# A Mamba-2 scan in transposed layout: the normalisation of each head group put off into the next group, and the decay matrices kept in three fixed tiles

## The chip, the cores and the metric

The kernel runs on one NeuronCore of a Trainium2 chip. The core has five engines that run side by side, each through its own instructions in order: TensorE (PE, matrix products), VectorE (DVE), ScalarE (ACT), GpSimd (POOL) and SyncE (SP, which issues the loads of the weights). They wait for one another by semaphores. The metric is the device time of one launch in microseconds, the median of several runs.

## The reference

A trunk of two layers on one sequence of 256 tokens, model width 1024, all in float32. Each layer is an FFN, a token mixer and another FFN, each followed by a layer norm. The mixer of the first layer is a sparse attention; that of the second is a Mamba-2 SSD, to which the change belongs:

```python
def ssd_mixer(x, w_in, conv_w, conv_b, dt_bias, a_log, d_skip, norm_g, w_out):
    z, xbc, dt = jnp.split(x @ w_in, [SSM_INNER, SSM_INNER + SSM_CONV_DIM], axis=-1)
    ...                                   # causal conv of 4 taps over xbc
    xs, b_in, c_in = jnp.split(jax.nn.silu(conv), [SSM_INNER, SSM_INNER + SSM_GROUPS * SSM_STATE], axis=-1)
    ...
    y = ssd_scan(xs, dt, a, b_in, c_in)
    y = y + xs * d_skip
    yz = y.reshape(bsz, seq, SSM_INNER) * jax.nn.silu(z)
    yz = yz.reshape(bsz, seq, SSM_GROUPS, SSM_INNER // SSM_GROUPS)
    yz = yz * lax.rsqrt(jnp.mean(jnp.square(yz), -1, keepdims=True) + RMS_EPS)
    return (yz.reshape(bsz, seq, SSM_INNER) * norm_g) @ w_out

# ssd_scan, inside a chunk of 128 tokens
seg = a_cs[..., :, None] - a_cs[..., None, :]
decay = jnp.exp(jnp.where(tri, seg, -jnp.inf))
cb = jnp.einsum('bclgn,bcsgn->bcgls', cm, bm)
y_diag = jnp.einsum('bcgrls,bcsgrp->bclgrp', cb[:, :, :, None] * decay, xdt)
```

The inner width is 2048: 32 heads of 64, in 4 groups of 8 heads; the state is 128, and 256 tokens make 2 chunks. Each group is normalised by its own root mean square.

## The kernel before

**Weights.** All products run as three float32r matmuls (`mm3`, L566 to L568): high half of the weights by high half of x, high by low, low by high. The weights stream from memory in units of 128 x 1024 floats. SP loads a raw unit (L268), ACT rounds it to the high half `wh` (L352, or L350 where a factor is folded in), DVE makes the low half `wl` as raw minus high (L380, L377). For the units in `W.by_dma` DVE is spared: ACT writes minus the high half into the low tile (L358), and an accumulating DMA that POOL issues adds the raw unit to it (L359). PE uses a unit when both halves are there.

**Tiles.** The raw units, and the scan's tiles of 128 x 1024 floats, come from one pool of 12 buffers (`f4`): the decay matrices M, the gate zT, the group's result yc, and a few more. A new tile takes over the buffer of an older one and waits until that has been read for the last time. In PSUM, `ptr` is a pool of two banks (transposes, the products of the scan, the sums of squares), `pmm` another of two.

**The scan.** Channels lie on the partitions and tokens along the row ("turned"), so that y needs no transposes before the output product. The loop over the four groups (from L1822) is written by hand as one row of calls; the order of the calls is the order on every engine. Between the steps of group g stand the fillers f[0] to f[7]: large products on PE, which are to cover what the other engines do. In groups 0 and 1 they are four tiles of the next group's x (`xs_tile`: projection, then a conv of one ACT and three DVE operations, L1596 and L1599, then a SiLU, L1591) and four tiles of the gate of the group after (`z_tile`: projection and a SiLU on ACT, L1561). In group 2 they are the x tiles of group 3 and four pieces of the output product (`out_piece`), in group 3 six further output pieces. A SiLU of x is held back in a list and issued at the next conv, or by `flush()`.

The steps of a group, in order:

- `x_tok`: eight transposes of x to token layout into two PSUM banks (L1677), times dt on DVE (`xdt`, L1679); `x_end`: `xe` on DVE (L1683).
- `decay_cbs`: the three decay matrices times C·B on DVE (L1653). Two of them stand at the end of the group before, the third here.
- `diag`: 48 matmuls of M by xdt and xe into two ptr banks (L1696), behind f[2] (f[1] in group 3). Then POOL loads the sums that the next group's decay is made of into two M tiles (`decay_load`, L1581).
- `gate`: DVE adds the skip term from the two banks (L1706) and multiplies by zT (L1711), into yc. `squares` on ACT (L1715), `square_sum` on DVE (L1720, L1721).
- `root`: four matmuls that sum the squares over the channels (PE, L1727), a copy by ACT (L1729), a power on POOL (L558).
- `decay_seg`: the next group's differences, on DVE (L1643), one for each chunk; the second writes into a third tile. `decay_exps`: a table load and three exponentials on ACT (L1649); the next SiLU loads its table again (L1561).
- `norm`: `spread` brings the root to all partitions (PE, L1736), DVE scales yc by it (L1745), ACT casts the high half of y (`yH`, L1748); `norm_low`: DVE makes the low half (`yL`, L1752). Both are read by the output product only.

Of the kernel before, what the change touches and what calls it, by code (L numbers as in the profile page):

```python
# [13 lines left out]
AF = mybir.ActivationFunctionType  # L14
# [422 lines left out]
def trunk_kernel(ctx: ExitStack, tc: tile.TileContext, widths, forms, x, ln_g, ln_b, wts, kvg, convp,  # L437
                 dt_bias, a_log, d_skip, norm_g, out):
    nc = tc.nc
# [10 lines left out]
    def nm(s):  # L450
        cnt[0] += 1
        return f"{s}_{cnt[0]}"

    def f4(s):
        return wk.tile([128, 1024], F32, name=nm(s), tag="f4", bufs=12)

    def f2(s):
        return wk.tile([128, 512], F32, name=nm(s), tag="f2", bufs=11)
# [29 lines left out]
    W = Weights(nc, f4, ring, wts, widths, forms, SLOTS, RAWS)  # L488
# [962 lines left out]
    def ssd(xT, u, ln_i):  # L1451
# [4 lines left out]
        scr = dram.tile([2, SH, 128], F32, name="scr")  # L1456

        p = nc.gpsimd
        ab, r, rr, s = (consts_w(n) for n in ("ab", "r", "rr", "s"))
        e = ab  # L1460
# [48 lines left out]
        for k in range(16):  # L1509
            W.scale[first_out + (2 * k if k < 4 else 3 + k)] = ng_sb[:, k:k + 1]  # L1510
        first_x = u + 10 + 8 + 4
        W.by_dma = {first_x + i for i in (1, 4, 6, 9, 12, 14)}
        spare[0] = 0

        def z0(t, c):
# [58 lines left out]
                                        zs[g][:, t * 512 + i * 128:t * 512 + (i + 1) * 128], ident)  # L1574
                nc.scalar.copy(zv[:, :, t, :], pt.rearrange("p (i l) -> p i l", i=4))

        M, E, xsT, pair, spareM = {}, {}, {}, [None], {}

        def decay_load(t, g):
            M[t, g] = f4("M")  # L1580
            nc.gpsimd.dma_start(M[t, g], scr[t:t + 1, g * 8:(g + 1) * 8, :].rearrange("o h l -> o (h l)")  # L1581
                                .to_broadcast([128, 1024]))
            if t:
                spareM[g] = f4("M")

        bT, cTt = f4("bT"), f4("cTt")
        late = []
# [1 line left out]
        def flush():  # L1589
            while late:  # L1590
                nc.scalar.activation(*late.pop(0), AF.Silu)  # L1591
# [19 lines left out]
        cbm = f4("cbm")  # L1611
        cbx = f2("cbx")
# [19 lines left out]
        def hv(ap):  # L1632
            return ap.rearrange("p (h d) -> p h d", h=8)
# [2 lines left out]
            return ap[:, g * 8:(g + 1) * 8][:, :, None].to_broadcast([128, 8, 64])  # L1636

        def decay_seg(t, g):
            src, dst = M[t, g], M[t, g]
            if t:  # L1640
                E[g] = src
                dst = M[t, g] = spareM.pop(g)
            nc.vector._custom_dve(TENSOR_ADD_SAT, out=dst.rearrange("p (h l) -> p h l", h=8),  # L1643
                                  in0=src.rearrange("p (h l) -> p h l", h=8),
                                  in1=acs[t][:, g * 8:(g + 1) * 8][:, :, None].to_broadcast([128, 8, 128]),
                                  s0=0.0, s1=LOWEST)

        def decay_exp(m):
            nc.scalar.activation(m, m, AF.Exp)  # L1649

        def decay_cb(m, c):
            mv = m.rearrange("p (h l) -> p h l", h=8)
            nc.vector.tensor_mul(mv, mv, c[:, None, :].to_broadcast([128, 8, 128]))  # L1653

        def decay_exps(g):
            for m in (M[0, g], E[g], M[1, g]):
                decay_exp(m)

        def decay_cbs(g, some=(0, 1, 2)):
            for i in some:  # L1660
                m, c = ((M[0, g], cbm[:, g * 128:(g + 1) * 128]), (E[g], cbx[:, g * 128:(g + 1) * 128]),
                        (M[1, g], cbm[:, 512 + g * 128:512 + (g + 1) * 128]))[i]
                decay_cb(m, c)

        yT = {}
        y, xe, yc, sq = {}, {}, {}, {}
# [14 lines left out]
        def x_end(g):  # L1681
            xe[g] = f2("xe")
            nc.vector.tensor_mul(hv(xe[g]), hv(y[0]), hb(dend, g))  # L1683

        def diag(g):

            m0, m1, e = M.pop((0, g)), M.pop((1, g)), E.pop(g)
            py = [ptr(), ptr()]
            for i in range(4):
                for t in range(2):  # L1690
                    prods = [(y[0], m0)] if not t else [(xe[g], e), (y[1], m1)]
                    for n, (a, m) in enumerate(prods):
                        for q in range(2):
                            h = 2 * i + q
                            c = (i % 2) * 256 + t * 128
                            nc.tensor.matmul(py[i // 2][q * 64:(q + 1) * 64, c:c + 128],  # L1696
                                             a[:, h * 64:(h + 1) * 64], m[:, h * 128:(h + 1) * 128],
                                             start=n == 0, stop=n == len(prods) - 1)
            return py

        def gate(g, py):
            yc[g] = f4("yc")
            sq[g] = [f2("sq"), f2("sq")]
            for b in range(2):
                for i in (2 * b, 2 * b + 1):
                    nc.vector.scalar_tensor_tensor(yc[g][:, i * 256:(i + 1) * 256], xsT[g][i],  # L1706
                                                   dsk[:, 4 * g + i:4 * g + i + 1],
                                                   py[b][:, (i % 2) * 256:(i % 2 + 1) * 256],
                                                   op0=ALU.mult, op1=ALU.add)
                c = slice(b * 512, (b + 1) * 512)  # L1710
                nc.vector.tensor_mul(yc[g][:, c], yc[g][:, c], zT[g][:, c])  # L1711

        def squares(g):
            for b in range(2):
                nc.scalar.activation(sq[g][b], yc[g][:, b * 512:(b + 1) * 512], AF.Square)  # L1715

        def square_sum(g):

            a, b = sq[g]
            nc.vector.tensor_add(a, a, b)  # L1720
            nc.vector.scalar_tensor_tensor(b[:, :256], a[:, :256], 4 * RMS_EPS, a[:, 256:], op0=ALU.add, op1=ALU.add)  # L1721

        def root(g):

            pt = ptr()
            for t in range(2):
                nc.tensor.matmul(pt[:, t:t + 1], sq[g][1][:, t * 128:(t + 1) * 128], mean, start=True, stop=True)  # L1727
            ms = tiny("ss")
            nc.scalar.copy(ms[:, :2], pt[:, :2])  # L1729
            return rsqrt_pool(ms[:, :2])  # L1730
# [9 lines left out]
        def norm(g, rs):  # L1740
            R = spread(rs)
            yT[g] = [(r2("yH"), r2("yL")) for _ in range(2)]
            vs = [yc[g][:, b * 512:(b + 1) * 512] for b in range(2)]
            for v in vs:
                nc.vector.tensor_mul(v.rearrange("p (i l) -> p i l", i=2), v.rearrange("p (i l) -> p i l", i=2),  # L1745
                                     R[:, None, :].to_broadcast([128, 2, 256]))
            for (H, L), v in zip(yT[g], vs):
                nc.scalar.copy(H, v)  # L1748

        def norm_low(g):  # L1750
            for b, (H, L) in enumerate(yT[g]):
                nc.vector.tensor_sub(L, yc[g][:, b * 512:(b + 1) * 512], H.bitcast(F32))  # L1752
# [63 lines left out]
        z_half(1, 1, 1, uz)  # L1816
        x_tok(0, 0)
        x_tok(1, 0)
        decay_exps(0)
        W.lows()  # L1820
        u += 4
        for g in range(SG):  # L1822
            if g < 2:
                f = [lambda i=i: xs_tile(g + 1, i, u + i) for i in range(4)]
                f += [lambda i=i: z_tile(g + 2, i, u + 4 + i) for i in range(4)]
            elif g == 2:
                x3 = [lambda i=i: xs_tile(3, i, u + 2 * i) for i in range(4)]
                o0 = [lambda i=i: out_piece(i, u + 2 * i + 1) for i in range(4)]
                f = [x3[0], x3[1], o0[0], x3[2], o0[1], x3[3], o0[2], o0[3]]
            else:  # L1830
                f = [lambda i=i: out_piece(4 + i, u + i) for i in range(6)]
            if g:
                x_tok(0, g)
                x_tok(1, g)
            x_end(g)
            if not g:
                decay_cbs(0, (0, 1))
                f[0]()
            decay_cbs(g, (2,))
            if g:  # L1840
                f[0]()
            else:
                z_turn(1)
            f[1]()
            if g == 3:
                py = diag(g)
                gate(g, py)
                squares(g)
                f[2]()
                square_sum(g)  # L1850
                f[3]()
                rs = root(g)
                f[4]()
                norm(g, rs)
                norm_low(g)
                f[5]()
                continue
            f[2]()
            py = diag(g)
            for t in range(2):  # L1860
                decay_load(t, g + 1)
            W.lows()
            gate(g, py)
            f[3]()
            squares(g)
            f[4]()
            square_sum(g)
            decay_seg(0, g + 1)
            f[5]()
            rs = root(g)  # L1870
            decay_seg(1, g + 1)
            f[6]()
            norm(g, rs)
            flush()
            decay_exps(g + 1)
            f[7]()
            norm_low(g)
            decay_cbs(g + 1, (0, 1))
            W.lows()
            u += 8  # L1880
        u += 6

# [9 lines left out]
    u, _ = ffn(xT, u, 5, last=True)  # L1892
# [36 lines left out]
```

## Time and profile before

| what | before |
|---|---|
| median of 3 runs | 1025.72 us (1023.33 to 1027.06) |
| the profiled execution | 1025.55 us, of which the span of the profile is 1023.8 us |
| mean granted clock of TensorE | 0.995 |
| PE busy over the span | 98% |
| DVE, ACT, POOL busy | 89%, 64%, 10% |
| read from HBM | 193.48 MB, 190 GB/s over the span |

The span is the time from the first to the last instruction in the profile; some 1.75 us of the execution lie around it. The second layer's mixer runs in the last third; its group loop stands at about 702 to 830 us. An engine's busy share is over the whole span. In the timelines of the trace, a row is a run of like instructions: start and duration in us, engine, line and operation, output from inputs, and in square brackets the idle time of that engine before it and what it waited for.

### The profile page before, as it was taken

To read this page: it belongs to the slowest core of one execution; us is meant where nothing else is said; L and a number is where in the kernel's file an instruction comes from. 1 tells how busy PE (TensorE), PEld (TensorE's weight loads), DVE (VectorE), ACT (ScalarE), POOL (GpSimd) and SP (SyncE) were. 2 spreads that over 40 slices of the span, in tenths; PEclk is the share of its full clock that TensorE was granted. 3 is DMA by queue.
4 is the path that set the end of the run, shared out by engine and by line. 5 is a ranking of instruction groups with operands and counts; after the bars stand their busy time and mean duration, and the time that the engine had idled before them with its cause. 6 is when DMAs were issued, how large, how long until landed. Compare 5 with 4: busy or idle time off the path is not lost.

```text
span 1023.8 us, 14877 instructions
## 1 busy us (share of the span) xinstructions
PE 1000.9 (98%) x5445; PEld 850.6 (83%) x5445; DVE 915.9 (89%) x1244; ACT 658.9 (64%) x951; POOL 103.6 (10%) x150
## 2 busy tenths in 40 slices
PE   9999999999999999999999999999988899999996
PEld 7878888898788888888888888999987688888885
DVE  6999998799899999989999998687788899999985
ACT  6776775476657776653786765587756545777670
POOL 0101101100000110001011000241010001010000
PEclk9999999999999999999999999999999999999998
DMA  9989999352639998873999886456755564999751
GB/s 338 276 248 288 295 277 343 108 166 83 206 106 257 254 271 283 281 274 96 274 260 260 264 291 226 165 159 174 226 193 176 205 227 106 287 295 285 211 194 42
DMA packets 64666, 229.62 MB, mean 224 GB/s; under 512 B 7280, under 2 KB 8112, under 8 KB 64592
## 3 DMA queue, kind: packets, MB, share of 16 engines
q1 hardware_dynamic: 52128, 183.95, 49.8%
q0 software_dynamic: 12464, 44.71, 21.5%
q8 instruction: 43, 0.70, 0.3%
q14 instruction: 31, 0.25, 0.1%
HBM read 193.48 MB, written 1.08 MB: 190 GB/s over the span
## 4 chain that ended last, share of the span: by engine, by line
PE 82%; DVE 7%; DMA 4%; ACT 4%; issue 2%; POOL 1%; SPq 0%; DVEq 0%; POOLq 0%
PE pmm L568 11%; PE pmm L567 11%; PE pmm L566 11%; PE acc L566 9%; PE acc L567 9%; PE acc L568 9%; DMA raw<-in_wts_dram 2%; PE ptr L567 2%; PE ptr L568 2%; PE ptr L566 2%; DVE wl L380 2%; PE pmm L733 1%; PE ptr L834 1%; DMA raw<-raw 1%; PE ptr L733 1%
## 5 line engine op out<-in xcount | busy, mean ns | idle before, releaser
L352 ACT CAST wh<-raw 128x1024 fp32r<-128x1024 f32 (+2 forms) x433 | 430.2, 1039 | 122.2 <-DVE raw L318 77.8
L380 DVE TENSOR_TENSOR wl<-raw,wh 128x1024 fp32r<-128x1024 f32 (+3 forms) x423 | 493.8, 1208 | 13.3 <-ACT wh L352 12.5
L566 PE MATMUL acc<-wh,hH 128*128 128x512 f32 (+1 forms) x352 | 138.0, 392 | 0.0
L567 PE MATMUL acc<-wl,hH 128*128 128x512 f32 (+1 forms) x352 | 136.7, 388 | 0.0
L568 PE MATMUL acc<-wh,hL 128*128 128x512 f32 (+1 forms) x352 | 136.6, 388 | 0.0
L566 PE MATMUL pmm<-wh,xT 128*128 128x512 f32 (+2 forms) x280 | 109.1, 390 | 0.1
L568 PE MATMUL pmm<-wh,xT 128*128 128x512 f32 (+2 forms) x280 | 107.5, 384 | 0.0
L567 PE MATMUL pmm<-wl,xT 128*128 128x512 f32 (+2 forms) x280 | 107.4, 384 | 0.0
L291 POOL DMA_DIRECT2D raw<-raw x59 | 50.9, 878 | 401.8 <-DVE raw L318 233.4
L567 PE MATMUL pmm<-wl,xf 128*128 128x512 f32 x224 | 87.3, 390 | 0.6 <-DVE wl L380 0.6
L566 PE MATMUL pmm<-wh,xf 128*128 128x512 f32 x224 | 87.9, 393 | 0.0
L568 PE MATMUL pmm<-wh,xf 128*128 128x512 f32 x224 | 87.3, 390 | 0.0
L318 DVE TENSOR_TENSOR raw<-raw,raw 128x1024 f32<-128x1024 f32 x69 | 82.9, 1219 | 0.4
L568 PEld LDWEIGHTS acc<-wh,hL 128*128 128x128 f32 x352 | 66.1, 188 | 13.7
L567 PEld LDWEIGHTS acc<-wl,hH 128*128 128x128 f32 x352 | 66.2, 188 | 13.5 <-DVE wl L380 0.6
L566 PEld LDWEIGHTS acc<-wh,hH 128*128 128x128 f32 x352 | 66.2, 188 | 12.8
L568 PEld LDWEIGHTS pmm<-wh,xT 128*128 128x128 f32 x280 | 52.6, 188 | 11.0 <-DVE xT L563 0.9
L567 PEld LDWEIGHTS pmm<-wl,xT 128*128 128x128 f32 x280 | 52.7, 188 | 10.1 <-DVE wl L380 0.7
L566 PEld LDWEIGHTS pmm<-wh,xT 128*128 128x128 f32 x280 | 52.6, 188 | 10.0 <-ACT xT L562 0.4
L567 PEld LDWEIGHTS pmm<-wl,xf 128*128 128x128 f32 x224 | 42.1, 188 | 9.6 <-DVE wl L380 1.1
L568 PEld LDWEIGHTS pmm<-wh,xf 128*128 128x128 f32 x224 | 42.0, 188 | 8.9
L566 PEld LDWEIGHTS pmm<-wh,xf 128*128 128x128 f32 x224 | 42.1, 188 | 8.6
(346 smaller groups left out, 1926.9 us busy)
## 6 DMA issues: line engine op xcount, KB each, us to landing
raw<-in_wts_dram SPq DMA_DIRECT2D x338, 512.0 KB, 5.3
raw<-raw POOLq DMA_DIRECT2D x59, 512.0 KB, 6.1
M<-scr POOLq DMA_DIRECT2D x8, 512.0 KB, 5.7
lng<-in_ln_g_dram POOLq DMA_DIRECT2D x6, 512.0 KB, 6.1
lnb<-in_ln_b_dram POOLq DMA_DIRECT2D x6, 512.0 KB, 5.3
wl<-raw POOLq DMA_DIRECT2D x6, 512.0 KB, 6.2
raw<-in_wts_dram SPq DMA_DIRECT2D x4, 408.0 KB, 6.9
raw<-in_wts_dram SPq DMA_DIRECT2D x4, 256.0 KB, 3.8
```

The costliest lines, as they stand in the source:

```text
L291: self.nc.gpsimd.dma_start(self.raw[r], self.raw[other], accum_op=ALU.add)
L318: self.nc.vector.tensor_add(self.raw[r], self.raw[r], self.raw[other])
L352: nc.scalar.copy(h[:, c:c + n], raw[:, c:c + n])
L380: self.nc.vector.tensor_sub(lo[:, s], raw[:, s], h[:, s].bitcast(F32))
L566: nc.tensor.matmul(ps, lh, rh, start=first, stop=False, skip_group_check=on)
L567: nc.tensor.matmul(ps, lh, rl, start=False, stop=False, skip_group_check=on)
L568: nc.tensor.matmul(ps, ll, rh, start=False, stop=last, skip_group_check=on)
L733: nc.tensor.matmul(ps, H[:, k * 128:(k + 1) * 128], xT.HL[:, k, :], start=k == 0, stop=False)
L834: nc.tensor.transpose(pt[:, i * 256 + t * 128:i * 256 + (t + 1) * 128], h[:, i * 128:(i + 1) * 128], ident)
```

## The change

The change has four parts.

- The normalisation of group g is put off into group g+1. `norm(g)` stands behind f[1] there (in group 3 ahead of f[1]), `norm_low(g)` behind the products and the decay loads (in group 3 behind the squares). Group 3 still normalises itself at its end.
- The decay is made one filler later. `decay_seg(0)` stands behind `root`, `decay_seg(1)` and the exponentials behind f[6]; all three multiplications by C·B stand at the start of the next group, behind `x_end`. A `flush()` behind f[4] and one behind f[6] issue a pending SiLU.
- The decay matrices stay in three tiles of their own for all groups. `M[0]` and `M[2]` are loaded, `M[1]` takes what the second `decay_seg` writes. Before, three fresh tiles came from the pool for each group.
- Two more units have their low halves made by accumulating transfers: offsets 18 and 22 are the second and the fourth x tile of group 3.

```diff
-        W.by_dma = {first_x + i for i in (1, 4, 6, 9, 12, 14)}
+        W.by_dma = {first_x + i for i in (1, 4, 6, 9, 12, 14, 18, 22)}
...
-        M, E, xsT, pair, spareM = {}, {}, {}, [None], {}
+        M, xsT, pair = [], {}, [None]
 
         def decay_load(t, g):
-            M[t, g] = f4("M")
-            nc.gpsimd.dma_start(M[t, g], scr[t:t + 1, g * 8:(g + 1) * 8, :].rearrange("o h l -> o (h l)")
+            if not M:
+                M.extend(f4("M") for _ in range(3))
+            nc.gpsimd.dma_start(M[2 * t], scr[t:t + 1, g * 8:(g + 1) * 8, :].rearrange("o h l -> o (h l)")
                                 .to_broadcast([128, 1024]))
-            if t:
-                spareM[g] = f4("M")
...
         def decay_seg(t, g):
-            src, dst = M[t, g], M[t, g]
-            if t:
-                E[g] = src
-                dst = M[t, g] = spareM.pop(g)
-            nc.vector._custom_dve(TENSOR_ADD_SAT, out=dst.rearrange("p (h l) -> p h l", h=8),
-                                  in0=src.rearrange("p (h l) -> p h l", h=8),
+
+            nc.vector._custom_dve(TENSOR_ADD_SAT, out=M[t].rearrange("p (h l) -> p h l", h=8),
+                                  in0=M[2 * t].rearrange("p (h l) -> p h l", h=8),
...
-            m0, m1, e = M.pop((0, g)), M.pop((1, g)), E.pop(g)
+            m0, m1, e = M
...
             x_end(g)
+            decay_cbs(g)
+            f[0]()
             if not g:
-                decay_cbs(0, (0, 1))
-                f[0]()
-            decay_cbs(g, (2,))
-            if g:
-                f[0]()
-            else:
                 z_turn(1)
-            f[1]()
             if g == 3:
-                py = diag(g)
-                gate(g, py)
-                squares(g)
+                norm(2, rs)
+                f[1]()
+                py = diag(3)
+                gate(3, py)
+                squares(3)
+                norm_low(2)
                 f[2]()
...
                 continue
+            f[1]()
+            if g:
+                norm(g - 1, rs)
             f[2]()
             py = diag(g)
             for t in range(2):
                 decay_load(t, g + 1)
+            if g:
+                norm_low(g - 1)
             W.lows()
             gate(g, py)
             f[3]()
             squares(g)
             f[4]()
+            flush()
             square_sum(g)
-            decay_seg(0, g + 1)
             f[5]()
             rs = root(g)
+            decay_seg(0, g + 1)
+            f[6]()
+            flush()
             decay_seg(1, g + 1)
-            f[6]()
-            norm(g, rs)
-            flush()
-            decay_exps(g + 1)
+            decay_exps()
             f[7]()
-            norm_low(g)
-            decay_cbs(g + 1, (0, 1))
-            W.lows()
             u += 8
```

On ACT, at the end of group 0 and the start of group 1, before (`wh`, `wl` are halves of weights, `zT` the gate, `xsT` the next group's x, `ss` the sums of squares):

```order
L1729 COPY ss_7272<-ptr_7269 128x2
L1561 ACTIVATE zT_7202<-pmm_7277 128x256
L352 CAST wh_7306<-raw_7153 128x1024
L358 ACTIVATE wl_7307<-wh_7306 128x1024
L1748 CAST yH_7314<-yc_7155 128x512
L1748 CAST yH_7316<-yc_7155 128x512
L1591 ACTIVATE xsT_7108<-cv_7189 128x256
L1649 ACT_TABLE_LOAD
L1649 ACTIVATE M_7147<-M_7147 128x1024
L1649 ACTIVATE M_7149<-M_7149 128x1024
```

and after:

```order
L352 CAST wh_7228<-raw_7078 128x1024
L1590 ACTIVATE xsT_7108<-cv_7186 128x256
L1561 ACTIVATE zT_7199<-pmm_7234 128x256
L352 CAST wh_7263<-raw_7116 128x1024
L1718 COPY ss_7269<-ptr_7266 128x2
L1561 ACTIVATE zT_7199<-pmm_7274 128x256
L352 CAST wh_7303<-raw_7150 128x1024
L358 ACTIVATE wl_7304<-wh_7303 128x1024
L1646 ACT_TABLE_LOAD
L1646 ACTIVATE M_6682<-M_6682 128x1024
L1646 ACTIVATE M_6684<-M_6684 128x1024
L1646 ACTIVATE M_6683<-M_6683 128x1024
```

The two casts `yH` have left this place, and the SiLU of `xsT` stands seven rows ahead of the exponentials' table load instead of right ahead of it, with two gate tiles in between.

On DVE, from the root of group 0 to the first conv tile of group 1, before (`ISA` is the custom operation of `decay_seg`):

```order
L1643 ISA M_7151<-M_7149,acs_6680 128x1024
L380 TENSOR_TENSOR wl_7267<-raw_7116,wh_7266 128x1024
L1745 TENSOR_TENSOR yc_7155<-yc_7155,ptr_7311 128x512 x2
L1752 TENSOR_TENSOR yL_7315<-yc_7155,yH_7314 128x512
L1752 TENSOR_TENSOR yL_7317<-yc_7155,yH_7316 128x512
L1653 TENSOR_TENSOR M_7147<-M_7147,cbm_6229 128x1024
L1653 TENSOR_TENSOR M_7149<-M_7149,cbx_6230 128x1024
L380 TENSOR_TENSOR wl_7355<-raw_7229,wh_7354 128x1024
L1679 TENSOR_TENSOR xdt_7369<-pxt_7364,dt_6218 128x512
L1679 TENSOR_TENSOR xdt_7376<-ptr_7371,dt_6218 128x512
L1683 TENSOR_TENSOR xe_7378<-xdt_7369,dend_6226 128x512
L1653 TENSOR_TENSOR M_7151<-M_7151,cbm_6229 128x1024
```

and after:

```order
L380 TENSOR_TENSOR wl_7229<-raw_7078,wh_7228 128x1024
L1639 ISA M_6682<-M_6682,acs_6678 128x1024
L380 TENSOR_TENSOR wl_7264<-raw_7116,wh_7263 128x1024
L1639 ISA M_6683<-M_6684,acs_6680 128x1024
L1668 TENSOR_TENSOR xdt_7348<-pxt_7343,dt_6218 128x512
L1668 TENSOR_TENSOR xdt_7355<-ptr_7350,dt_6218 128x512
L1672 TENSOR_TENSOR xe_7357<-xdt_7348,dend_6226 128x512
L1652 TENSOR_TENSOR M_6682<-M_6682,cbm_6229 128x1024
L1652 TENSOR_TENSOR M_6684<-M_6684,cbx_6230 128x1024
L1652 TENSOR_TENSOR M_6683<-M_6683,cbm_6229 128x1024
```

The norm (`yc` by `ptr`), its lows `yL` and two multiplications by `cbm` and `cbx` no longer stand between `decay_seg` and `xdt`; the three multiplications stand behind `xe` in one block.

Further on in group 1, on DVE after the change, from the second conv tile to the gate:

```order
L1598 SCALAR_TENSOR_TENSOR cv_7426<-pxs_7401,convp_sb,cv_7426 128x253
L1734 TENSOR_TENSOR yc_7152<-yc_7152,ptr_7437 128x512 x2
L1598 SCALAR_TENSOR_TENSOR cv_7474<-pxs_7448,convp_sb,cv_7474 128x255
L1598 SCALAR_TENSOR_TENSOR cv_7474<-pxs_7448,convp_sb,cv_7474 128x254
L1598 SCALAR_TENSOR_TENSOR cv_7474<-pxs_7448,convp_sb,cv_7474 128x253
L380 TENSOR_TENSOR wl_7435<-raw_7301,wh_7434 128x1024
L1741 TENSOR_TENSOR yL_7441<-yc_7152,yH_7440 128x512
L1741 TENSOR_TENSOR yL_7443<-yc_7152,yH_7442 128x512
L380 TENSOR_TENSOR wl_7484<-raw_7338,wh_7483 128x1024
L1695 SCALAR_TENSOR_TENSOR yc_7519<-xsT_7023,dsk,ptr_7486 128x256 x2
```

Here are the norm and the lows of group 0 (`yc_7152`), each ahead of the gate of group 1 (`yc_7519`), which takes its input from the two ptr banks.

On POOL, from the M loads of group 1 to those of group 3, before:

```order
L1581 DMA M_7517<-scr 128x1024
L1581 DMA M_7519<-scr 128x1024
L558 TENSOR_TENSOR rs_7643<-ss_7641,mhalf 128x2
L1581 DMA M_7868<-scr 128x1024
L1581 DMA M_7870<-scr 128x1024
```

and after:

```order
L1582 DMA M_6682<-scr 128x1024
L1582 DMA M_6684<-scr 128x1024
L359 DMA wl_7595<-raw_7432 128x1024
L558 TENSOR_TENSOR rs_7638<-ss_7636,mhalf 128x2
L359 DMA wl_7763<-raw_7628 128x1024
L1582 DMA M_6682<-scr 128x1024
L1582 DMA M_6684<-scr 128x1024
```

Two more accumulating transfers (L359) stand on this queue, the first behind the M loads that group 1 issues, the second ahead of those of group 2; the M loads now go to the same two tiles each time.

More of the change, by code (lines that the diff above doesn't have):

```diff
@@ L1638, in decay_seg, with decay_exps, decay_cbs @@
         def decay_seg(t, g):
-            src, dst = M[t, g], M[t, g]
-            if t:
-                E[g] = src
-                dst = M[t, g] = spareM.pop(g)
-            nc.vector._custom_dve(TENSOR_ADD_SAT, out=dst.rearrange("p (h l) -> p h l", h=8),
-                                  in0=src.rearrange("p (h l) -> p h l", h=8),
+            nc.vector._custom_dve(TENSOR_ADD_SAT, out=M[t].rearrange("p (h l) -> p h l", h=8),
+                                  in0=M[2 * t].rearrange("p (h l) -> p h l", h=8),
                                   in1=acs[t][:, g * 8:(g + 1) * 8][:, :, None].to_broadcast([128, 8, 128]),
                                   s0=0.0, s1=LOWEST)
[L1648 to L1663, printed above, removed]
+        def decay_exps():
+            for m in (M[0], M[2], M[1]):
+                nc.scalar.activation(m, m, AF.Exp)
+        def decay_cbs(g):
+            for m, c in ((M[0], cbm[:, g * 128:(g + 1) * 128]), (M[2], cbx[:, g * 128:(g + 1) * 128]),
+                         (M[1], cbm[:, 512 + g * 128:512 + (g + 1) * 128])):
+                mv = m.rearrange("p (h l) -> p h l", h=8)
+                nc.vector.tensor_mul(mv, mv, c[:, None, :].to_broadcast([128, 8, 128]))
         yT = {}
@@ L1818, in ssd @@
         x_tok(1, 0)
-        decay_exps(0)
+        decay_exps()
         W.lows()
@@ L1835, in ssd @@
             x_end(g)
+            decay_cbs(g)
+            f[0]()
             if not g:
-                decay_cbs(0, (0, 1))
-                f[0]()
-            decay_cbs(g, (2,))
-            if g:
-                f[0]()
-            else:
                 z_turn(1)
-            f[1]()
             if g == 3:
-                py = diag(g)
-                gate(g, py)
-                squares(g)
+                norm(2, rs)
[4 more added lines that the diff above has]
+                norm_low(2)
                 f[2]()
-                square_sum(g)
+                square_sum(3)
                 f[3]()
-                rs = root(g)
+                rs = root(3)
                 f[4]()
-                norm(g, rs)
-                norm_low(g)
+                norm(3, rs)
+                norm_low(3)
                 f[5]()
                 continue
+            f[1]()
+            if g:
+                norm(g - 1, rs)
             f[2]()
@@ L1866, in ssd @@
             f[4]()
+            flush()
             square_sum(g)
-            decay_seg(0, g + 1)
             f[5]()
             rs = root(g)
+            decay_seg(0, g + 1)
+            f[6]()
+            flush()
             decay_seg(1, g + 1)
-            f[6]()
-            norm(g, rs)
-            flush()
-            decay_exps(g + 1)
+            decay_exps()
             f[7]()
-            norm_low(g)
-            decay_cbs(g + 1, (0, 1))
-            W.lows()
             u += 8
```

## Prediction

> **What bounds the kernel now.** I read the page first, then the windows of the scan stage and of what follows it, then the waits of TensorE (PE) inside the scan, and at last the timelines around each wait.
>
> ```profile
> span 1023.8 us, 14877 instructions
> PE 1000.9 (98%) x5445; PEld 850.6 (83%) x5445; DVE 915.9 (89%) x1244; ACT 658.9 (64%) x951; POOL 103.6 (10%) x150
> PE 82%; DVE 7%; DMA 4%; ACT 4%; issue 2%; POOL 1%; SPq 0%; DVEq 0%; POOLq 0%
> ...
> 702.00:830.00 128.00, 116.30 (x901) 106.42 (x900) 108.54 (x147) 82.87 (x112) 10.79 (x16) 0.99 0.62 202
> 750.00:760.00 10.00, 7.43 (x57) 7.25 (x56) 9.82 (x16) 5.58 (x10) 1.83 (x3) 0.92 0.54 211
> 760.00:770.00 10.00, 10.00 (x79) 9.92 (x77) 7.87 (x10) 6.86 (x9) 0.00 (x0) 0.90 0.58 200
> 830.00:1017.00 187.00, 185.23 (x874) 154.00 (x872) 170.96 (x206) 112.07 (x150) 16.39 (x20) 1.00 0.67 205
> ```
>
> PE is busy for 1000.9 of 1023.8 us; 22.9 us is idle. The group loop of the scan stands at 702 to 830, and there alone PE idles 128.00 − 116.30 = 11.7 us. After it PE is busy 185.23 of 187 us, so whatever the scan gains or loses, the rest only moves along. The columns behind the counts are the granted clock, the DMA share and GB/s: the clock falls to 0.92 and 0.90 in two slices, which is 0.08 × 10 + 0.10 × 10 = 1.8 us of clock.
>
> ```profile
> PE ptr L1727 <- DVE sq L1721: 3.7, 2, 2.6
> PE pmm L566 <- ACT zT L1561: 1.7, 1, 1.7
> PE pxt L1677 <- ACT xsT L1591: 1.6, 1, 1.6
> PE ptr L1696 <- DVE M L1653: 1.4, 2, 0.7
> PE pmm L1677 <- ACT xsT L1591: 1.2, 1, 1.2
> PE ptr L1696 <- ACT wh L350: 1.1, 1, 1.1
> PE ptr L1696 <- DVE xe L1683: 1.0, 2, 0.8
> ```
>
> These rows (total, times, longest) sum to 11.7 us: all that PE loses in the scan is ten waits on DVE's or ACT's in-order rows. The change touches each of them. So the question is which go, and what is late next.
>
> **The change, part by part.** *The end of group 0.* PE and ACT there:
>
> ```profile
> 727.62 0.61 PE L1736 MATMUL ptr<-ident,rs 128*128 128x128 f32 x4
> ...
> 733.03 0.33 PE L1677 MATMUL pxt<-ident,xsT 128*128 128x128 f32 x1 [1.60 <-ACT xsT L1591]
> ...
> 731.45 1.21 ACT L1748 CAST yH<-yc 128x512 fp32r<-128x512 f32 x2 [1.21 <-DVE yc L1745]
> 732.57 0.41 ACT L1591 ACTIVATE xsT<-cv 128x256 f32<-128x256 f32 x1
> 733.00 1.28 ACT L1649 ACT_TABLE_LOAD   x1
> 734.29 2.95 ACT L1649 ACTIVATE M<-M 128x1024 f32<-128x1024 f32 x3
> ```
>
> The last SiLU of the next group's x (732.57) stands behind the two yH casts, and these behind DVE's norm. Now it is flushed two fillers earlier, so PE's gap of 1.60 goes. The casts leave too, and with them most of ACT's 1.21 of idle: the table load can begin at about 730.2 instead of 733.00, after the −high of the transferred unit, and the three exponentials end 2.75 earlier. The spread (727.62, 0.36 to the next start) goes to the next group, and comes back there from the one before; over all it is neither saved nor added.
>
> ```profile
> 728.46 1.23 DVE L1643 CUSTOM_DVE_ANT_1 M<-M,acs 128x1024 f32<-128x1024 f32 x1 [2.31 <-issue]
> ...
> 730.73 1.28 DVE L1745 TENSOR_TENSOR yc<-yc,ptr 128x512 f32<-128x512 f32 x2
> 732.10 1.29 DVE L1752 TENSOR_TENSOR yL<-yc,yH 128x512 fp32r<-128x512 f32 x2
> 735.38 1.23 DVE L1653 TENSOR_TENSOR M<-M,cbm 128x1024 f32<-128x1024 f32 x1 [1.99 <-ACT M L1649]
> ...
> 739.91 1.23 DVE L380 TENSOR_TENSOR wl<-raw,wh 128x1024 fp32r<-128x1024 f32 x1 [2.17 <-ACT wh L352]
> 741.05 0.68 DVE L1679 TENSOR_TENSOR xdt<-pxt,dt 128x512 f32<-128x512 f32 x1
> ```
>
> DVE stands idle here for 2.31 + 1.99 + 2.17 = 6.5 us, while PE's next transposes are already done; in this order xdt waits until 741.05 behind work that waits for ACT. With norm, its lows and the cbs out of the way, xdt runs as soon as PE gives it, at 731.1. Rows lie 1.14 apart where one has 1.23 (739.91 to 741.05), so I price a large DVE row at 1.14 and the pairs of 1.28 and 1.29 at 1.2.
>
> *Group 1, up to the root.*
>
> ```profile
> 743.08 0.44 PE L1696 MATMUL ptr<-M,xe 128*64 128x128 f32 x4 [0.28 <-DVE xe L1683]
> ...
> 758.01 0.58 PE L1727 MATMUL ptr<-mean,sq 128*128 128x1 f32 x4 [2.57 <-DVE sq L1721]
> ```
>
> From xdt (741.05) to the end of the square sum (757.87, just ahead of 758.01) DVE takes 16.8 us, of which 0.46 idle: 16.4 of work. The new order adds ahead of that square sum two cbs (2.28), one weight low that used to stand earlier (1.14), the norm of group 0 (1.2) and its lows (1.2): 22.2. From 731.1 that ends at 753.3. Two waits on ACT are new: the first conv tile stands behind the exponentials (1.3), another behind the yH casts (1.25, of the kind of 731.45). The square sum ends at 755.8 and PE's root starts at 755.9: **2.1 earlier** than 758.01. Of PE's own waits, the 0.28 and a 0.70 at the diagonal products go, since the M tiles are ready near 736.4, ahead of the products' 740.4. In their place stands a new wait: of the two ptr banks that the products take, one holds the spread, until DVE's norm has read it, at about 742.9, where PE wants it at 741.7: up to 1.2. Ahead of the root PE then waits 1.8 to 2.6 (before 2.57).
>
> That gap is where the clock falls: the slices at 750 and 760 are the only slow ones, right behind it, while 1.60 and 1.71 of idle did not lower it. My gap lies between, and each row that comes later than laid out makes it longer, so I leave the 1.8 us of clock in. [...]
>
> *Groups 2 and 3.*
>
> ```profile
> 774.05 0.68 DVE L1679 TENSOR_TENSOR xdt<-pxt,dt 128x512 f32<-128x512 f32 x1
> ...
> 790.30 0.58 PE L1727 MATMUL ptr<-mean,sq 128*128 128x1 f32 x4 [1.13 <-DVE sq L1721]
> ...
> 798.46 0.33 PE L1677 MATMUL pmm<-ident,xsT 128*128 128x128 f32 x1 [1.17 <-ACT xsT L1591]
> ...
> 804.96 0.68 DVE L1679 TENSOR_TENSOR xdt<-pmm,dt 128x512 f32<-128x512 f32 x1
> ...
> 814.19 0.43 DVE L1721 SCALAR_TENSOR_TENSOR sq<-sq 128x256 f32<-128x256 f32 x1
> ...
> 816.07 0.50 PE L1727 MATMUL ptr<-mean,sq 128*128 128x1 f32 x4
> ```
>
> Group 2 starts 2.5 earlier (2.1, and the spread's 0.36). DVE's chain was 16.1 (774.05 to 790.16). One low goes to a transfer (−1.14), two cbs (2.28), norm (1.2), lows (1.2) and one weight low (1.2) come in ahead: 20.8. It starts at 764.7 instead of 774.05, so the square sum is ready at 785.5 and PE, which is there at about 786.0, does not wait: the 1.13 goes. The wait of 1.71 for zT (behind the exponentials) falls to about 0.8, as they begin earlier. The root is 4.3 earlier than 790.30. The products' second bank is free at 775.1, 0.75 ahead of its need.
>
> Group 3 starts 4.6 earlier. At its head 1.17 goes (its SiLU is flushed early) and so do 1.09 + 0.76 + 0.70 ahead of and in the products, 3.72 in all. Coming in: about 0.35 for the last M tile, 1.1 for the spread's bank and 0.36 for the spread: 1.81. The square sum then ends at 809.5 (before 814.5), and root(3) starts at 809.6 against 816.07: **6.5 earlier**. Behind that nothing changes but the norm of group 3, which stays.
>
> *The two further transfers.*
>
> ```profile
> 741.31 1.06 ACT L358 ACTIVATE wl<-wh 128x1024 fp32r<-128x1024 f32 x1
> ...
> 726.17 72.82 SPq L268 DMA_DIRECT2D raw<-in_wts_dram  x20
> ...
> raw<-in_wts_dram SPq DMA_DIRECT2D x43, 512.0 KB, 4.5
> ...
> wl<-raw POOLq DMA_DIRECT2D x5, 512.0 KB, 6.1
> ```
>
> Each adds 1.06 us on ACT and a transfer on POOL's queue, and takes 1.14 from DVE. ACT works 82.87 of 128 us, so 2.1 more is hidden unless a SiLU or a square stands behind it; uncovered it costs 2.1. The transfers land 6.1 after issue, and I have both landing over 5 us ahead of their product. POOL issues them between the M loads, whose tiles are wanted 10 us later.
>
> *The kept tiles.* Three M tiles are held for good and yc lives a group longer, so the f4 tiles that the weights rotate through are fewer, and the load of a unit waits until the buffer of the fifth before it is read, for a transferred one until its transfer has landed. Loads come 72.82 / 20 = 3.6 us apart, five in 18.2; a transferred unit holds its buffer for 4.5 + 1.04 or so + 1.06 + 6.1 = 12.7. That leaves 5.5 us, and 3.6 at the tightest unit as I lay the new order over the old times. I cost it at nothing; the cover is these 3.6 us.
>
> *Sum.* Against the profiled execution of 1025.55 us (its span is 1023.8, and it lies 0.17 under the median of the runs, which I leave out): 1025.55 − 6.5 = **1019.0**. What I priced as unknown: the clock (0 to −1.8), the bank waits (2.3 in all, from 0 to as much as a norm that comes 1 us later in three groups), ACT's two −highs (0 to 2.1).
>
> **Rivals.** *The clock does not fall* (the idle time that lowers it lies between 1.71 and 2.57 in this trace, and my gap may be under it): 1019.0 − 1.8 = 1017.2. For it: 1.8 is close to 1.71; against it: every unforeseen wait on DVE lengthens this gap.
>
> *DVE keeps the chain.* The same rows go through DVE, 1.2 more of norm, 1.2 of lows and 2.28 of cbs now in front of each square sum instead of behind it. If ACT hands over conv tiles and yH some 1.2 later in each of three groups than laid out, the bank is late in group 2 too and the root's waits come back: 3 × 1.2 = 3.6 less gain, 1022.6. For it: DVE is 85% busy in the stage (108.54 of 128) and each cover I counted is 0.4 to 0.8. Against it: the 6.5 us of idle at the head of group 1, which these rows now fill.
>
> *The weights' ring turns too slowly (slower).* If loads or transfers land later, the casts wait for raw tiles at the three units behind a transferred one. It decides from landings 3.6 us over the 4.5 (8.1 us): below that nothing, above it three casts late by what is over. To lose the 6.5 us and 5.5 more takes 12 us, so 4 at each: landings of 12.1, and the time would be 1031. Against it: the DMA share of the stage is 0.62, and neither of the two medians (4.5 and 6.1) is near.
>
> *It doesn't do what it says*: put-off work only moves the waits, one for one (a bank wait for a SiLU wait): 1025.5. I count this as the far end of the second rival.
>
> **How the numbers follow.** Forecast 1019.0: 0.42, its own range 1017.8 to 1020.8. Clock kept: 0.20 (1017.2, to 1015.5 where the bank waits vanish also). DVE keeps the chain: 0.32 (1022.6, from 1020.6 to 1025.5). Ring: 0.06 (1031). The range from 1015.5 to 1024.5 holds the first two and most of the third. About 0.5%, 5.1 us, is what a measurement of this kernel can tell from no change: faster is below 1020.6. That takes nearly all of the forecast and of the clock rival: 0.61. Within: the third and a rest of the first, 0.33. Slower: 0.06.
>
> **What would show it.** Right: no wait of the transposes for xsT in groups 1 to 3; xdt of group 1 near 731; roots near 755.9, 786 and 809.6; DVE's idle between 725 and 741 mostly gone; new waits at the products on DVE's norm, at 741 and 800, near 1 us. Wrong: root(1) at 758 or later (DVE keeps the chain); casts that wait for raw DMAs (ring); a half clock in another place, or two of them; PE waits on wl that a transfer made.

## The result and the profile after

The changed kernel takes 1018.38 us (median of 4 runs, 1017.52 to 1019.94), the one before 1026.39 us (4 runs, 1023.33 to 1027.17). The ratio is 0.9929, with a 95% interval of 0.9905 to 0.9954: faster, by 0.5 to 1%. The profiled execution took 1019.94 us (span 1018.2), the slowest of its four; that before took 1025.55 (span 1023.8).

The page of the kernel after, and the windows that answer to those of before (after the counts stand the granted clock, the DMA share and GB/s):

```profile
span 1018.2 us, 14875 instructions
PE 1001.6 (98%) x5445; PEld 851.9 (84%) x5445; DVE 913.2 (90%) x1242; ACT 661.3 (65%) x953; POOL 106.4 (10%) x152
...
702.00:824.00 122.00, 116.26 (x897) 107.26 (x896) 105.07 (x145) 85.02 (x114) 13.68 (x18) 0.97 0.71 219
750.00:760.00 10.00, 7.52 (x46) 7.35 (x46) 8.52 (x12) 5.30 (x9) 2.48 (x2) 0.77 0.85 250
760.00:770.00 10.00, 9.59 (x73) 9.39 (x72) 5.96 (x7) 8.34 (x10) 0.00 (x0) 0.89 0.45 146
824.00:1011.00 187.00, 185.38 (x875) 154.06 (x873) 170.96 (x206) 112.11 (x150) 16.12 (x20) 1.00 0.66 204
```

The group loop takes 122 us instead of 128, with PE as long busy (116.26 against 116.30); what follows it is the same. So nearly the whole difference is PE's idle time in the loop, 5.7 us against 11.7. (The loop starts 0.5 us earlier after, so the two windows are not cut at quite the same work.) The granted clock, though, is lower than before: 0.77 and 0.89, which is 0.23 × 10 + 0.11 × 10 = 3.4 us, where it was 1.8.

PE's waits in the loop (total, times, longest), and the rows of its timeline at them and at the roots:

```profile
PE ptr L1716 <- DVE sq L1710: 3.0, 2, 2.5
PE ptr L1685 <- DVE yc L1734: 2.4, 2, 1.4
PE pmm L566 <- ACT zT L1561: 0.4, 1, 0.4
...
742.50 0.44 PE L1685 MATMUL ptr<-M,xdt 128*64 128x128 f32 x4 [0.99 <-DVE yc L1734]
...
755.34 0.90 PE L1716 MATMUL ptr<-mean,sq 128*128 128x1 f32 x4 [2.48 <-DVE sq L1710]
...
786.57 0.50 PE L1716 MATMUL ptr<-mean,sq 128*128 128x1 f32 x4
...
802.49 0.44 PE L1685 MATMUL ptr<-M,xdt 128*64 128x128 f32 x4 [1.39 <-DVE yc L1734]
...
810.16 0.58 PE L1716 MATMUL ptr<-mean,sq 128*128 128x1 f32 x4 [0.47 <-DVE sq L1710]
```

Of the ten waits before, those for xsT, for xe, for M and for wh are gone. In their place stand two that did not exist, in groups 1 and 3: the products (L1685) wait for DVE's norm (L1734), which still has to read the spread from the bank that they take. The root of group 1 waits as long as before (2.48 against 2.57), only earlier. On DVE, at the head of group 1:

```profile
730.59 0.69 DVE L1668 TENSOR_TENSOR xdt<-pxt,dt 128x512 f32<-128x512 f32 x1 [2.59 <-PE pxt L1666]
...
737.08 1.52 DVE L1598 SCALAR_TENSOR_TENSOR cv<-pxs,convp_sb,cv 128x255 f32<-128x255 f32 x3 [1.20 <-ACT cv L1595]
...
743.51 1.51 DVE L1598 SCALAR_TENSOR_TENSOR cv<-pxs,convp_sb,cv 128x255 f32<-128x255 f32 x3 [1.15 <-ACT cv L1595]
```

DVE now waits for PE's transposes (2.59) where it used to be late for them, and xdt comes at 730.59 instead of 741.05.

### The profile page after: what moved, and what is told of

Read it like the earlier page. It is cut to its first block, busy times and chain, and to the rows that moved or that the text cites. A ratio compares the mean times of both kernels' runs of the same rounds, so it can differ in the third digit from the quotient of the medians.

```text
span 1018.2 us, 14875 instructions
## 1 busy us (share of the span) xinstructions
PE 1001.6 (98%) x5445; PEld 851.9 (84%) x5445; DVE 913.2 (90%) x1242; ACT 661.3 (65%) x953; POOL 106.4 (10%) x152
## 4 chain that ended last, share of the span: by engine, by line
PE 85%; DVE 6%; ACT 3%; issue 2%; DMA 2%; POOL 1%; SPq 0%; DVEq 0%; ACTq 0%; POOLq 0%
PE pmm L566 12%; PE pmm L568 12%; PE pmm L567 12%; PE acc L566 9%; PE acc L568 9%; PE acc L567 9%; PE ptr L567 2%; PE ptr L568 2%; PE ptr L566 2%; DVE wl L380 2%; PE pmm L733 1%; PE ptr L834 1%; DMA raw<-raw 1%; PE ptr L733 1%; PE pxs L566 1%
```

## The experiments

All were timed in five rounds against the kernel before on the same chip; ratios are to that kernel, with their 95% intervals. e1 to e4, e5 to e8 and e9 to e12 ran on three different chips, so kernels of different groups are better compared by their ratios than by their times.

**e1, the two further transfers taken back.**

```diff
-        W.by_dma = {first_x + i for i in (1, 4, 6, 9, 12, 14, 18, 22)}
+        W.by_dma = {first_x + i for i in (1, 4, 6, 9, 12, 14)}
```

> The changed kernel with the two further transfers taken back (their lows on DVE again). Theory (the gain is in the order at the heads of groups 1 to 3): the two lows cost DVE 1.2 each in group 2, whose square sum then ends at 787.3 to 788.5 where PE comes at 786.6; 0.5 to 2 us over the changed kernel, 1019 to 1020.5. Rival (the gain is DVE work taken away): 3 us or more over it, 1021.5 and up.

Measured: 1019.43 us, ratio 0.9937 (0.9921 to 0.9952). The time is as the theory has it, and not to be told from the changed kernel's. Its mechanism did not show: in the profile PE does not wait at the root of group 2, and only a bank wait of 0.28 us at that group's products is new.

**e2, fresh tiles.** `decay_load` takes three new f4 tiles for each group.

```diff
-            if not M:
-                M.extend(f4("M") for _ in range(3))
+            if not t:
+                L[:] = [f4("M"), None, None]
+            else:
+                L[2] = f4("M")
...
+            if t:
+                L[1] = f4("M")
```

> The changed kernel with three fresh tiles for each group's decay instead of three kept ones. Theory: the tiles alone are worth 0 to 1 us (the second difference waits for the transfer that landed at 728.35 before, and that stands 1.5 us behind its new place, with exponentials of the other two tiles ahead of it): 1018 to 1019.5. Rival (the kept tiles are the gain: 2.31 us of DVE idle were this wait): 2 us or more over the changed kernel, 1020.5 and up.

Measured: 1018.77 us, ratio 0.9926 (0.991 to 0.9942). Also as the theory has it: beside the other parts, the kept tiles are worth nothing that can be told.

**e3, the norm at home.**

```diff
-                norm(2, rs)
                 f[1]()
...
                 squares(3)
-                norm_low(2)
                 f[2]()
...
             f[1]()
-            if g:
-                norm(g - 1, rs)
             f[2]()
...
-            if g:
-                norm_low(g - 1)
...
             decay_seg(1, g + 1)
+            norm(g, rs)
             decay_exps()
             f[7]()
+            norm_low(g)
```

> The changed kernel with the norm and its lows back in their own group (behind the second difference and f[7]); the later decay, the early SiLU, kept tiles and transfers stay. Theory (the decay's multiplications ahead of xdt and the late SiLU were the cost, not the norm): the bank waits of 1.0 and 1.4 go, yL ahead of xdt costs about as much; 1016.5 to 1020. Rival (the put-off norm is the gain): 3 us or more back, 1021.5 and up.

Measured: **1015.6 us**, ratio 0.9897 (0.9878 to 0.9916), no run over 1016.13. The median lies below the theory's range, which began at 1016.5. Every run is faster than the fastest of the changed kernel (1017.52), though the intervals of the two ratios overlap a little. PE's waits in the loop, its root of group 1, and DVE at the head of group 1:

```profile
PE pmm L566 <- ACT zT L1561: 1.4, 1, 1.4
PE ptr L1685 <- DVE M L1652: 1.3, 2, 0.7
PE ptr L1716 <- DVE sq L1710: 1.3, 1, 1.3
PE ptr L1716 <- ACT cv L1595: 0.6, 1, 0.6
...
753.46 0.58 PE L1716 MATMUL ptr<-mean,sq 128*128 128x1 f32 x4 [1.27 <-DVE sq L1710]
...
730.76 1.29 DVE L1741 TENSOR_TENSOR yL<-yc,yH 128x512 fp32r<-128x512 f32 x2 [1.02 <-ACT yH L1737]
731.97 0.68 DVE L1668 TENSOR_TENSOR xdt<-pxt,dt 128x512 f32<-128x512 f32 x1
```

With the norm back ahead of it, xdt comes at 731.97, 1.4 later than in the changed kernel. But DVE has no norm and no lows between xdt and the square sum, the bank is free, and the root stands at 753.46 instead of 755.34, though the loop began 0.5 later here. So putting off the norm to the place that the change gives it is a loss of some 3 us, inside a change that gains.

Two things make up this loss in the profiled executions (1019.94 and 1016.02 us), and the larger is the clock: PE idles 5.8 us in the loop of the changed kernel and 4.6 in that of e3, while the clock lost is 3.4 us there and nothing here (1.00 over 702 to 824). With six transfers the same move is worth less: e12 below is 1.6 us faster than e1, and their intervals overlap.

**e4, the decay where it was.** The differences one filler earlier, two multiplications back at the group's end, and the flush behind f[4] taken out (e10 takes out that flush alone).

```diff
-            decay_cbs(g)
-            f[0]()
             if not g:
+                decay_cbs(0, (0, 1))
+                f[0]()
+            decay_cbs(g, (2,))
...
             f[4]()
-            flush()
             square_sum(g)
+            decay_seg(0, g + 1)
             f[5]()
             rs = root(g)
-            decay_seg(0, g + 1)
+            decay_seg(1, g + 1)
             f[6]()
             flush()
-            decay_seg(1, g + 1)
             decay_exps()
             f[7]()
+            decay_cbs(g + 1, (0, 1))
+            W.lows()
```

> The changed kernel with the decay where it was before (differences one filler earlier, two multiplications at the group's end, ahead of xdt, no SiLU flushed early but the one behind f[6]); the put-off norm, kept tiles and transfers stay. Theory: xdt of group 1 stands behind two multiplications that wait for exponentials until 734, so it comes near 734.5 instead of 730.6, the roots 2 to 4 us later in each group: 1021.5 to 1024.5. Rival (the put-off norm is the gain): 1020 or less.

Measured: 1021.37 us, ratio 0.9956 (0.9942 to 0.9971), just below the theory's range and over the rival's. PE at the products and the root of group 1, and the clock behind it:

```profile
745.40 0.44 PE L1685 MATMUL ptr<-M,xdt 128*64 128x128 f32 x4 [2.95 <-DVE yc L1734]
...
758.24 0.58 PE L1716 MATMUL ptr<-mean,sq 128*128 128x1 f32 x4 [2.48 <-DVE sq L1710]
...
756.00:760.00 4.00, 1.76 (x15) 1.79 (x16) 3.97 (x5) 2.81 (x5) 1.61 (x2) 1.00 0.73 251
760.00:764.00 4.00, 4.00 (x36) 4.00 (x35) 2.37 (x3) 2.14 (x4) 0.00 (x0) 1.00 0.63 121
```

DVE, delayed by the multiplications that wait for the exponentials (4.53 us of idle), comes later to everything. xdt comes at 738.20 and not at 734.5 as I expected, since a weight low ahead of it waits 2.17 us for ACT; the bank wait grows from 0.99 to 2.95 and the root moves from 755.34 to 758.24.

**e5, e6, e7: the root later, the norm later, both.** e5 moves `root` behind f[6] in groups 0 to 2; e6 moves the put-off norm and its lows behind the next square sum, where nothing waits for the banks; e7 does both. For e5,

```diff
-            rs = root(g)
             decay_seg(0, g + 1)
             f[6]()
+            rs = root(g)
             flush()
```

and, for e6,

```diff
-                norm(2, rs)
                 f[1]()
...
-                norm_low(2)
                 f[2]()
                 square_sum(3)
+                norm(2, rs)
+                norm_low(2)
...
             f[1]()
-            if g:
-                norm(g - 1, rs)
             f[2]()
...
-            if g:
-                norm_low(g - 1)
...
             square_sum(g)
+            if g:
+                norm(g - 1, rs)
+                norm_low(g - 1)
             f[5]()
```

> The changed kernel with the root one filler later (behind f[6] instead of f[5]) in groups 0 to 2; its result is wanted only by the norm in the next group. Theory (DVE's chain to the square sum sets the root, and PE's 2.48 of waiting and the half clock behind it follow from where root stands): the wait ahead of root(1) and the half clock go, the two bank waits (1.0 and 1.4) stay; 1013.5 to 1016. Rival (the chain is late for the next step too, and the wait turns up behind: at the bank, at the gate tiles): 1017.5 or more.

> The changed kernel with the put-off norm and its lows still later: behind the next group's square sum, where the products' banks are free. Theory (the put-off norm costs through the bank that its spread holds and through 2.4 us on DVE ahead of the square sum): both bank waits go, the wait ahead of root(1) falls from 2.48 to near 1.2, no half clock; 1013 to 1016. Rival (it was the decay's place alone, the norm's place is indifferent): 1017.5 or more.

> Both: root one filler later and the put-off norm behind the next square sum. Theory: all waits on the square sum and on the bank go, some 0.5 to 1 for zT and the M tiles stays: 1011.5 to 1014. Rival: no better than the better of the two alone, 1014.5 or more.

Measured: e5 1014.55 us, ratio 0.9882 (0.9868 to 0.9895); e6 1012.9 us, 0.9868 (0.9855 to 0.9882); e7 **1012.38 us**, 0.9864 (0.9849 to 0.9879). PE's waits in the loop, of e5, of e6 and of e7 in turn:

```profile
PE ptr L1685 <- DVE yc L1734: 2.0, 2, 1.4
PE pmm L566 <- ACT zT L1561: 0.6, 1, 0.6
PE ptr L1716 <- DVE sq L1710: 0.5, 1, 0.5
```

```profile
PE pmm L566 <- ACT zT L1561: 0.8, 1, 0.8
PE ptr L1685 <- DVE M L1652: 0.6, 1, 0.6
PE ptr L1716 <- DVE sq L1710: 0.4, 1, 0.4
```

```profile
PE ptr L1685 <- DVE M L1652: 0.5, 1, 0.5
PE pmm L566 <- ACT zT L1561: 0.4, 1, 0.4
```

e5 and e7 came in within the theory's ranges, e6 0.1 us under its own: its wait ahead of the root of group 1 fell to 0.44 us, not only to near 1.2. No half clock shows in the three loops (1.00 over 702 to 824 in each). Putting the norm off does pay, if it is put off far enough: with the norm behind the square sum, PE idles 1.8 us in the loop, and 0.9 with the root moved too (5.8 in the changed kernel). e7 is faster than the kernel before and than the changed one; whether it is faster than e6 the intervals do not tell.

**e8, the early SiLU alone**, in the kernel before.

```diff
             f[4]()
+            flush()
             square_sum(g)
```

> The kernel before with one edit: a flush of the pending SiLU behind f[4]. Theory (xsT's SiLU is one cause among several; xdt still stands behind the multiplications that wait for the exponentials): the waits of 1.60 and 1.17 for xsT go, but DVE starts xdt no earlier, so the root waits longer by most of it; 0 to 2 us gained, 1024 to 1026. Rival (the late SiLU alone was the loss): 3 us or more gained, 1023 or less.

Measured: 1024.6 us, ratio 0.9977 (0.9965 to 0.9989). Some of PE's waits:

```profile
PE ptr L1727 <- DVE sq L1721: 3.7, 2, 2.6
PE ptr L1696 <- DVE xdt L1679: 2.2, 2, 1.1
PE ptr L1696 <- DVE xe L1683: 1.5, 2, 0.8
```

The wait of 1.60 for xsT is gone, but PE now waits 1.15 for xdt at the products of group 1, a wait that was not there; the root waits as before. (The other 1.10 for xdt, in group 3, stands where 1.09 was put down to ACT's wh before. The xsT wait of 1.17 stayed: the last x tile of group 3 is f[5] of group 2, behind this flush.) The medians differ by 2 us, under the 3 that would have made the SiLU the cause. The profile does not show even that gain: PE's idle in the loop falls from 11.7 to 11.4 us, and the profiled execution took 1025.69 us where that of the kernel before took 1025.55. Where the 2 us come from stays open.

**e9, the decay's new place and the flushes alone**: norm at home, fresh tiles, six transfers (the diffs of e1, e2 and e3 together).

> The kernel before with the decay's new place and the two early flushes alone: norm at home, fresh tiles, six transfers. Theory (the decay's multiplications no longer ahead of xdt are the gain; kept tiles and transfers were worth 1 us or less each): 1015.5 to 1018. Rival (tiles and transfers carry it once the norm is at home): 1020 or more.

Measured: 1020.28 us, ratio 0.9941 (0.9928 to 0.9954). Against e8, which has the flush behind f[4] alone, the decay's place and the flush behind f[6] are worth some 4 us. But my theory fell, and the time is in the rival's range: e9 is 4.7 us over e3. Where it lost them: DVE's gate in group 1 of e9, POOL's transfer ahead of it and its landing (KB, us), PE's root; then the same gate in e3.

```profile
749.16 0.87 DVE L1701 SCALAR_TENSOR_TENSOR yc<-xsT,dsk,ptr 128x256 f32<-128x256 f32 x2 [2.92 <-PE pmm L568]
...
741.34 0.88 POOL L359 DMA_DIRECT2D wl<-raw  x1 [10.28 <-DVE cv L1602]
...
wl<-raw POOLq DMA_DIRECT2D x1, 512.0 KB, 7.7
...
756.09 0.73 PE L1722 MATMUL ptr<-mean,sq 128*128 128x1 f32 x4 [4.28 <-DVE sq L1716]
```

```profile
746.53 0.87 DVE L1695 SCALAR_TENSOR_TENSOR yc<-xsT,dsk,ptr 128x256 f32<-128x256 f32 x2
```

The timeline names a matmul as what ended the 2.92, but that has nothing to do with yc. The waits in the program have it: this yc takes over the buffer of the raw unit that the transfer reads, and waits for that transfer too; 741.34 + 7.7 is 749.0, where the gate starts. In e3 the yc takes over the buffer of a unit whose low DVE made itself, and does not wait. The 2.31 of DVE idle at 728.46 in the kernel before is of the same kind, with a decay tile: POOL issued a transfer at 721.94, and it landed 6.4 us later. The root's wait in e9 is 3.0 us longer than in e3, and the half clock behind it (0.57 over 756 to 760, 1.00 in e3) costs 1.7 more; the two profiled executions are 4.3 us apart.

**e10, without the flush behind f[4].**

```diff
             f[4]()
-            flush()
             square_sum(g)
```

> The changed kernel without the flush behind f[4]; the one behind f[6], ahead of the exponentials, stays. Theory (behind f[6] the SiLU still comes a filler ahead of the transposes, since no yH cast stands before it): the same within 1 us, 1017.5 to 1019.5. Rival (the early flush removes the waits of 1.60 and 1.17): 1020 or more.

Measured: 1020.12 us, ratio 0.9937 (0.9922 to 0.9951). The median is over the range that I gave and in the rival's, the ratio that of the changed kernel within its interval. The rival's mechanism does not show: PE has no wait for xsT here either, so the flush behind f[6] does for that. Whether the early one is worth 1 us stays open.

**e11, another bank for the spread of group 1.**

```diff
-        def spread(rs):
+        def spread(rs, own=False):
...
-            pt = ptr()
+            pt = psum.tile([128, 512], F32, name=nm("pxt"), tag="acc11", bufs=1) if own else ptr()
...
-            R = spread(rs)
+            R = spread(rs, g == 0)
```

> The changed kernel with group 1's spread in another bank (that of the first transposes, free by then), so that the products find both ptr banks free. Theory (in group 1 DVE's chain to the square sum sets the end): the bank wait of 1.0 goes and the wait ahead of root(1) grows by as much, to 3.4; no gain, 1017.5 to 1020. Rival (the bank wait is a loss of its own): 1 us gained, 1017.4 or less.

Measured: 1020.24 us, ratio 0.9934 (0.992 to 0.9948): no gain, and 0.2 us over the theory's range. The root of group 1:

```profile
756.12 0.98 PE L1716 MATMUL ptr<-mean,sq 128*128 128x1 f32 x4 [3.69 <-DVE sq L1710]
```

The bank wait of 0.99 is gone and has turned up ahead of the root, 3.69 instead of 2.48. In group 1 it cost nothing of its own; DVE's chain sets the root.

**e12, e3 with six transfers**, to part the kept tiles from the transfers in e9.

> The kernel of e3 (norm at home, later decay, kept tiles) with six transfers in place of eight. Theory (in e9 the tile of group 1's result took over the buffer of a raw unit whose accumulating transfer landed at 749.08, and DVE's gate waited 2.92 us for it; with kept tiles it takes another one): the gate does not wait, the wait ahead of root(1) is near 1.3 instead of 4.28, and two lows cost 1 us or less; 1015.5 to 1017.5. Rival (the two transfers are what e9 lacked): 1019 or more.

Measured: 1017.87 us, ratio 0.9924 (0.9902 to 0.9945), between e3 and e9 and 0.4 us over the theory's range. The root of group 1:

```profile
753.06 0.58 PE L1716 MATMUL ptr<-mean,sq 128*128 128x1 f32 x4 [1.28 <-DVE sq L1710]
```

The mechanism is as told: the wait is 1.28 instead of 4.28, with the kept tiles as the difference from e9. The time is not as clear, since its runs go from 1015.86 to 1019.44 and the interval touches that of e9 and of e3. How the 4.7 us between e9 and e3 divide into tiles and transfers stays open.

## Why the prediction was right, and where it was not

**The sum.** 1019.0 was forecast and 1018.38 measured; the profiled execution fell by 5.6 us where I had 6.5. That the two numbers agree to 0.6 us is in part luck: the sum starts from one execution of 1025.55, the median before is now 1026.39, and the medians fell by 8.0 us. In the profile the stations came out close: xdt of group 1 at 731.1 forecast, 730.59 measured; the roots at 755.9, 786.0 and 809.6, measured 755.34, 786.57 and 810.16. Some 0.5 of that is not the change: before, the loop's first transposes started at 702.33, after, at 701.78, from the stages ahead.

**The new waits.** The spread's bank was priced at up to 1.2 in group 1 and 1.1 in group 3 (0.99 and 1.39 measured), with none in group 2 (none). The wait ahead of root(1) at 1.8 to 2.6: 2.48. zT's was to fall from 1.71 to 0.8: 0.41. The wait of 0.47 ahead of root(3) I did not have, and the 0.35 for the last M tile did not come. DVE's idle between 725 and 741, which was to be mostly gone, is 3.8 us (2.59 and 1.20) of 6.5.

**The clock** is the mis-sized term. I left the 1.8 us in; the profiled execution lost 3.4, in one stretch behind the root of group 1:

```profile
754.00:756.00 2.00, 0.66 (x4) 0.69 (x4) 1.97 (x4) 2.00 (x4) 0.89 (x1) 0.86 0.43 152
756.00:758.00 2.00, 2.00 (x11) 2.00 (x11) 2.00 (x3) 0.24 (x2) 1.48 (x1) 0.50 1.03 270
758.00:760.00 2.00, 2.00 (x11) 2.00 (x11) 0.66 (x1) 0.00 (x0) 0.10 (x1) 0.50 1.11 197
760.00:762.00 2.00, 2.00 (x11) 2.00 (x10) 0.00 (x0) 0.40 (x2) 0.00 (x0) 0.50 0.76 225
762.00:764.00 2.00, 2.00 (x17) 2.00 (x17) 1.05 (x1) 1.98 (x2) 0.00 (x0) 0.94 0.73 227
```

Half clock from about 755.4 to 762.1. The profiled run was the slowest of four, with a mean clock of 0.993; the others had 0.996 to 0.998, so they lost less clock. How much is lost after this wait differs between profiled runs: with the same 2.48 us ahead of the root, e4 and e10 lost nothing (1.00 over 756 to 764), and e9, with 4.28 us, lost 1.7 (0.57 over 756 to 760). The rival in which the clock does not fall, at 1017.2, was therefore a matter of the run. An estimate from the mean clocks: e10's run without half clock has 0.997, so the two runs of the changed kernel with 0.997 and 0.998 (1017.52 and 1018.02 us) probably had none either, and the median of 1018.38 lies between runs with the half clock and runs without.

**The price of the put-off norm** is the step that was wrong in substance, though the sum held. I took the norm, its lows and the multiplications by C·B out of xdt's way together, and counted their return on DVE as the cost of one move. e4 and e3 show two moves of opposite sign: the decay's later place gains some 3 us, and the norm where the change puts it loses some 3. My 2.4 us of norm and lows ahead of each square sum were the loss, with the 3.4 us of clock that the profiled run lost behind the wait of 2.48 ahead of the root; for xdt they were worth 1.4. The bank, which I priced as a loss of its own, cost nothing in group 1 (e11); in group 3 that was not tried. That e6 gains 5.5 us over the changed kernel by moving the same rows behind the square sum says it again.

**The SiLU.** I let the 1.60 for xsT count as a gain of its own. e8 shows that alone most of it turns into a wait for xdt (1.15 in group 1), so that PE's idle falls by only 0.3 us.

**Kept tiles and transfers** at nothing: right beside the other parts (e1, e2). But the cover was not the load ring alone. Which tile takes over the buffer of a transferred unit changes with every allocation, and in e9 that cost DVE 2.92 us. The rival of the slow ring did not come: the loads' median landing between 702 and 830 went from 4.4 to 4.8 us, and no wait of PE is put down to them.

**DVE keeps the chain**, the second rival, was in part what happened in group 1, where the root waits as before; e5 shows it by moving the root away from the chain, some 4 us faster.

## What to carry to other kernels

- When work is put off to take it out of one chain, look which chain it joins at its new place. It must go behind the step that someone waits for; two rows of 1.2 us ahead of that step, with the 3.4 us of clock that the profiled run lost behind it, cost more here than they gained, and behind it the put-off norm gained 2.7 us over the norm at home (e6 against e3).
- Undo the parts of a winning change one at a time: one of the four here was a loss, and the best kernel (1012.38 us) came from putting it right and moving the root.
- A step whose result is wanted late, like the root once the norm is put off, should itself move off the chain that feeds it.

## What the runs showed of the hardware that was not expected

- The length of PE's idle time did not tell how much clock would be lost behind it. 2.48 us ahead of the root of group 1 was followed by 6.8 us of half clock in the changed kernel's profiled run and by none in e4's and e10's (1.00 over 756 to 764); 4.28 us in e9 was followed by 1.7 us of clock lost (0.57 over 756 to 760). In e4 another 2.95 us, ahead of the products of group 1, also passed at 1.00 (over 702 to 824), and in e8 the clock was 0.79 over 804 to 808 and 0.78 over 808 to 812, where PE waited 1.10, 0.76 and 0.69 us. So the bound that the prediction read from one trace, between 1.71 and 2.57 us of idle, did not hold in the other runs; what decides is not shown by them.
- A releaser in the profile can be wrong by kind: DVE's 2.92 was laid to a matmul, and 2.31 to nothing ("issue"), where both ended with the landing of an accumulating transfer that still read the buffer (at 749.0 in e9, at 728.3 in the kernel before).
